# Operand tiles on multiples of 512 bytes, and an expert layer's routing arithmetic in smaller pieces

## Chip, cores and metric

One of the cores of a Trainium2 chip runs the kernel. The metric is the time of one execution on the device, in microseconds (us). The kernel before takes 1301.25 us, the median of 3 runs (1300.66 to 1303.61).

## The reference

A trunk of two layers over 272 tokens (16 meta tokens and 256 of the input) of 1024 features, all in float32:

```python
for i in range(DEPTH):
    hn = rms_norm(h, mix_norm_g[i])
    h = h + (conformer_conv(hn, ...) if i % 2 == 0 else multiscale_pool(hn, ...))
    hn = rms_norm(h, ffn_norm_g[i])
    h = h + (swiglu(hn, ...) if i % 2 == 0 else moe_swiglu(hn, ...))
return rms_norm(h[:, N_META:], final_norm_g)
```

Layer 0 has a convolution module (two projections around a depthwise convolution of 31 taps) and a dense SwiGLU of width 2816. Layer 1 has a pooling mixer and a mixture of experts: a router picks the best 2 of 8 experts for each token, each expert is a SwiGLU of width 3584, and the two results are added with softmax weights. The experts' weights are 352 MB of the 402 MB that the weight queue loads.

## The kernel before

**Precision.** TensorE multiplies in a form of float32 that keeps fewer bits (float32r). A weight tile `raw` of 2048 columns (1 MB) is therefore cut in two units of 1024; ScalarE casts each into `w_hi` (line 105, `Weights.hi`), and VectorE subtracts, `w_lo = raw - w_hi` (line 128, `Weights.lo`). Activations are split likewise, and a product is three matmuls: high by high, low by high, high by low. A few units of the experts are left `plain`: they are multiplied straight from `raw` as float32.

**Dense part.** In layer 0 the weights are the stationary operand and the activations the moving one. `xh` and `xl` (lines 317 and 318) hold 8 chunks of 272 columns, one behind the other, 1088 bytes each; `sh` and `slo` (line 539) and `gh` and `gl` (line 631, 11 chunks each) do the same for later stages. `column` (line 336) multiplies one tile of weights with all chunks by `mm3` (line 311, whose matmuls are lines 313 to 315).

**Expert part.** Here the tokens of an expert are stationary (`x0b` to `x6b` for the big experts 0 to 4 with room for 128 tokens, `x0s` to `x6s` for the small ones 5 to 7 with room for 64) and 512 columns of weights move. The work is 56 steps, one for each expert and each 512 of its 3584 columns, listed in `steps` (line 220): the first 7 are expert 0's (of which the first `ALONE` = 6 and the last `QUIET` = 3 of all steps are fixed as big ones), then steps of big and small experts mostly alternate. A step projects to gate and up (`project`, line 1156, matmuls in lines 1167, 1171 and 1173), and between them does the down projection of the step before (`down`, line 1228, lines 1236 to 1239; `weave`, line 1429). A step of a big expert has 36 + 24 matmuls of 512 columns and 4 float32 ones, one of a small expert 32 + 16.

**The order of the side work.** `side` (line 1141) is a list of small functions. `beside` (line 1143) is called after every second chunk of a projection and every second of a down projection, that is 10 times in a step (6 times in step 0, which has no step before it): it frees a weight unit, runs the first function of `side`, and then writes the subtraction of the next units to VectorE's queue. So a function of `side` stands on VectorE between two `w_lo` subtractions, and its length decides how late the next one is. At most 4 cast units are ahead (`W_BUFS`). In each step one slot goes to the low part of the turned activations (`flip_later`, line 1198, puts it in front).

The experts 1 to 7 are ordered by how many tokens they have: `places` (line 902) ranks them and writes their numbers (`ids_i`), `count_most` (line 920) the largest count, `by_place` (line 931) reorders positions and weights, and `weights_of_tokens` (line 948) makes the softmax weights. Then for each expert `assign` builds a matrix P of ones and zeros (line 1005), `factors` multiplies it with the tokens' factors (line 1075), and `known` copies the result out. In step 0 the slots hold: factors and ranking of expert 0's and all places (slots 1 and 2), the counts (slot 3), the weights (4), the assign of expert 1 (5), its factors (6). At the start of step `SUMS_FROM` = 4, six functions are put in front of the list: for each half t of the tokens the sum of high and low features (line 1386) and `gains(t)` (line 1372: four products into the one buffer `x_of`, then a store to `x_rows` in HBM from POOL's queue), then `freed`, then `rows_of_tokens` (line 959, 14 instructions). POOL gathers the rows of a later expert from `x_rows` (`fetch`, lines 1019 and 1347); that of expert 5 (`BIG`) at the start of step 5.

SP issues all weight loads in the order in which their buffers are freed (line 85). It reads the experts' numbers into registers at step `IDS_AT` = 1 (line 1358); all engines read the largest count at step `COUNT_AT` = 2.

Of the kernel before, what the change touches and what calls it, by code (L numbers as in the profile page):

```python
# [6 lines left out]
F32 = mybir.dt.float32  # L7
F32R = mybir.dt.float32r
# [4 lines left out]
OP = mybir.AluOpType  # L13
# [5 lines left out]
T = SEQ + META  # L19
# [17 lines left out]
DG, SOONER, SUMS_LAG = 8, 12, 2  # L37
ABOUT = 5
LINE = 16
ALONE, IDS_AT, COUNT_AT, SUMS_FROM, QUIET = 6, 1, 2, 4, 3  # L40
PLAIN_AT = 6
BIG, CAP, SMALL_CAP = 5, 128, 64
TURN_AT = {False: 4, True: 2}
# [123 lines left out]
def body(tc, xT, w_pw1, w_pw2, w_gu, w_dn, w_pool, m_gate, m_up, m_down, small, moe_g,  # L167
# [7 lines left out]
    def pool(stack, name, bufs=1, **kw):  # L175
        return stack.enter_context(tc.tile_pool(name=name, bufs=bufs, reuse_waits="tile", **kw))
# [101 lines left out]
    for t in iw[1:]:  # L278
# [5 lines left out]
    POOL.iota(token[:, :2], pattern=[[128, 2]], base=0, channel_multiplier=1,  # L284
              allow_small_or_imprecise_dtypes=True)
    g1 = consts.tile([128, KC], F32)

    def table(func):

# [24 lines left out]
        PE.matmul(ps, lhsT=w[0], rhs=x[1], start=False, stop=False)  # L314
        PE.matmul(ps, lhsT=w[1], rhs=x[0], start=False, stop=last)  # L315

    xh = act.tile([128, KC, T], F32R, name="xh")
    xl = act.tile([128, KC, T], F32R, name="xl")
    rstd = act.tile([128, T], F32, name="rstd")
    ssq = act.tile([128, T], F32, name="ssq")  # L320

    def split(hi, lo, src):
        ACT.copy(hi, src)
# [40 lines left out]
    with ExitStack() as cs:  # L364
# [5 lines left out]
        pstat = pool(cs, "cst", 1, space=PSUM)  # L370
        u = cv.tile([128, KC, T], F32, name="u")
        v = cv.tile([128, KC, T], F32, name="v")

        warm(psum.tile([128, T], F32, name="mm")[:, :128], WARM[5])
        table(AF.Sqrt)
# [160 lines left out]
        sums()  # L536
        dgs.close()
        sx = pool(cs, "sx", side="right")
        sh = sx.tile([128, KC, T], F32R, name="sh")
        slo = sx.tile([128, KC, T], F32R, name="slo")  # L540

        d2 = tmp.tile([128, T], F32, name="hn")
        ACT.activation(d2, mu, AF.Square)
# [81 lines left out]
    with ExitStack() as cs:  # L625
# [2 lines left out]
        psum = pool(cs, "fps", 3, space=PSUM)  # L628
        pstat = pool(cs, "fst", 1, space=PSUM)
        ppool = pool(cs, "fpt", 2, space=PSUM)  # L630
        gh = ff.tile([128, FH, T], F32R, name="gh")
        gl = ff.tile([128, FH, T], F32R, name="gl")
        ms = pstat.tile([128, T], F32, name="ms")
        sl = {}

# [43 lines left out]
        for s in range(2):  # L679
# [7 lines left out]
            for m in range(KC):  # L687
# [24 lines left out]
                if s == 1 and m in POOL_AFTER[:-1]:  # L712
# [11 lines left out]
        rst = po.tile([128, 3], F32, name="rst")  # L724
        rsqrt(rst, st, 0, ff, 3)
        yh, yl = (t.rearrange("p k t -> p (k t)")[:, :2 * D].rearrange("p (b d) -> p b d", b=2)
                  for t in (xh, xl))
        def weigh(g, src):

            d = slice(g * 256, g * 256 + 256)  # L730
# [171 lines left out]
    def places(scratch):  # L902
# [17 lines left out]
    def count_most(scratch):  # L920
        hot, cmp = (squares_of(scratch, i, 1)[:, 0] for i in range(2))
        most = scratch[:, 0:1]
        shape = [128, n_rest, n_rest]
# [5 lines left out]
        DVE.tensor_copy(cnt_i, most)  # L929

    def by_place(dst, src, scratch):

# [12 lines left out]

    wt = rt.tile([128, 2, 2], F32, name="wt")

    def weights_of_tokens(scratch):
        den = rt.tile([128, 2], F32, name="den")
        DVE.tensor_scalar(den, ex, 1.0, None, op0=OP.add)  # L950
        DVE.reciprocal(wt[:, :, 0], den)
        DVE.tensor_mul(wt[:, :, 1], wt[:, :, 0], ex)
        for t in range(2):
            DVE.tensor_scalar(rc[:, t], oh[:, t, 0], wt[:, t, 0:1], None, op0=OP.mult)
            DVE.scalar_tensor_tensor(rc[:, t], oh[:, t, 1], wt[:, t, 1:2], rc[:, t],
                                     op0=OP.mult, op1=OP.add)
        by_place(rcq[:, :, :, 2], rc, scratch)

    def rows_of_tokens(scratch):


        small, room = (scratch[:, i * NE:(i + 1) * NE] for i in range(2))
        has, row = (scratch[:, 32 + 16 * i:48 + 16 * i].rearrange("p (t e) -> p t e", t=2)
                    for i in range(2))
        t4, t4b = (scratch[:, 64 + 32 * i:96 + 32 * i].rearrange("p (t k e) -> p t k e", t=2, k=2)
                   for i in range(2))
        r4, m4 = (scratch[:, 128 + 4 * i:132 + 4 * i].rearrange("p (t k) -> p t k", t=2)
                  for i in range(2))
        s2, s4 = [128, 2, NE], [128, 2, 2, NE]
        DVE.tensor_scalar(small, place_of, float(BIG), None, op0=OP.is_ge)  # L970
# [3 lines left out]
        DVE.scalar_tensor_tensor(room, small, float(BIG * (CAP - SMALL_CAP) - CAP), room,  # L974
                                 op0=OP.mult, op1=OP.add)
        DVE.scalar_tensor_tensor(row, posm, -1.0, room[:, None].to_broadcast(s2),
                                 op0=OP.add, op1=OP.add)
        DVE.tensor_scalar(small, place_of, float(BIG - 1), None, op0=OP.not_equal)
        DVE.tensor_tensor(has, has, small[:, None].to_broadcast(s2), op=OP.mult)
        DVE.tensor_tensor(t4, oh, has[:, :, None].to_broadcast(s4), op=OP.mult)  # L980
# [53 lines left out]
    class Expert:  # L1034
# [47 lines left out]
        def fetch(self, rows):  # L1082
            self.rows = rows
            fetch_rows(rows, self.q, self.width)
# [49 lines left out]

    with ExitStack() as cs:
        ws = pool(cs, "mw", 2)
        pm = pool(cs, "mpm", 2, space=PSUM)
        pg_pool = pool(cs, "mpg", 1, space=PSUM)
        pu_pool = pool(cs, "mpu", 1, space=PSUM)
# [185 lines left out]
        for i, t in enumerate(gain1):  # L1325
            nc.gpsimd.dma_start(t, bass.AP(tensor=moe_g.tensor, offset=moe_g.offset + i * 256,
                                           ap=[[0, 128], [1, 256]]))
        table(AF.Silu)
        side += [lambda: experts[0].factors(2),
                 lambda: (experts[0].known(2), places(scratch)),  # L1330
                 lambda: (count_most(scratch), by_place(posq, posm, scratch)),
                 lambda: weights_of_tokens(scratch)]
        before = lambda: None
        for q in range(1, NE):
            e = experts[q] = Expert(q, ws, pm)
            side += [lambda e=e, before=before: (before(), e.assign(posq)), e.factors]
            before = e.known
            if q == BIG - 1:
                before = lambda e=e: (e.known(), e.back())
        side.append(before)  # L1340
# [4 lines left out]
        prev, py_of, n_fetched = None, {}, 0  # L1345

        def fetch(q):
            experts[q].fetch(fetched_rows[n_fetched % 2])

        for n_step, (q, f) in enumerate(steps):  # L1350
            e = experts[q]
# [16 lines left out]
            if n_step == SUMS_FROM:  # L1368
# [15 lines left out]
                pieces = []  # L1384
                for t in range(2):
                    pieces += [lambda t=t: DVE.tensor_add(yacc[:, t], xth[:, t].bitcast(F32),
                                                          xtl[:, t].bitcast(F32)),
                               lambda t=t: gains(t)]
# [202 lines left out]
```

## Time and profile before

| | before |
|---|---|
| time, median of 3 runs | 1301.25 us |
| the profiled execution: its time, and its span from first to last instruction | 1302.38 us, 1300.2 us |
| TensorE matmuls, share of the span | 98% |
| VectorE, ScalarE | 84%, 71% |
| moved to and from HBM, mean | 318 GB/s |
| granted clock of TensorE, mean | 0.994 |

A row of the profile names the engine (PE is TensorE, DVE is VectorE, ACT is ScalarE, POOL is GpSimd; PEld its weight loads; SPq and the like the queues' own instructions), the line of the kernel, the operation, and the tiles written and read. Matmuls are pipelined, so that the time from one start to the next, not the length given for one, is what a matmul takes of TensorE. "<-" names what ended a wait.

### The profile page before, as it was taken

Reading aid. Unit: us, or ns where it says so; the run is one execution under the profiler, and the core shown is the slowest. Engines: PE = TensorE matmul, PEld = TensorE weight load, DVE = VectorE, ACT = ScalarE, POOL = GpSimd, SP = SyncE. Lnnn points to the kernel's source line nnn. Section 1 sums busy time; section 2 is a strip of 40 time slices with the busy share of each in tenths; the row PEclk is TensorE's granted clock in tenths of the full one; section 3 lists DMA queues with packets and bytes.
Section 4 is the critical chain, followed back from the end, with each engine's and each line's share of the span. In section 5 each row is a group of like instructions: output and inputs, shape, how many; then the busy total and the mean of one; then the engine's idle time right before and its main releaser. Section 6 shows DMA issues by size and latency. Waiting matters only on the chain.

```text
span 1300.2 us, 19132 instructions
## 1 busy us (share of the span) xinstructions
PE 1272.4 (98%) x6655; PEld 1038.2 (80%) x6655; DVE 1096.6 (84%) x1471; ACT 927.5 (71%) x1263; POOL 22.4 (2%) x37
## 2 busy tenths in 40 slices
PE   9999999999989999999999999999999999999995
PEld 8988999999977767777777777777777777777773
DVE  7997886666677788999899998899989998999876
ACT  6765644445564657888688878888878887888764
POOL 0000000000010010000000000000000000000010
PEclk9999999999998999999999999999999999999998
DMA  9800435523867889999999799999999999999971
GB/s 364 310 15 1 142 134 199 203 88 139 317 251 282 319 325 366 419 420 420 409 410 413 283 406 421 420 421 420 419 377 392 422 420 422 374 422 421 419 298 36
DMA packets 61401, 414.22 MB, mean 319 GB/s; under 512 B 6896, under 2 KB 7536, under 8 KB 14320
## 3 DMA queue, kind: packets, MB, share of 16 engines
q1 hardware_dynamic: 58032, 402.22, 77.4%
q0 software_dynamic: 1872, 6.55, 1.4%
q10 hardware_dynamic: 1392, 4.14, 0.8%
q8 instruction: 54, 0.88, 0.3%
q14 instruction: 51, 0.42, 0.1%
HBM read 407.90 MB, written 4.98 MB: 318 GB/s over the span
## 4 chain that ended last, share of the span: by engine, by line
PE 91%; DVE 3%; DMA 3%; ACT 1%; issue 1%; SPq 0%; ACTq 0%; DVEq 0%
PE pu L1167 11%; PE pg L1167 10%; PE mm L315 7%; PE mm L313 7%; PE mm L314 7%; PE pg L1173 6%; PE pu L1173 6%; PE pyb L1239 5%; PE pyb L1236 5%; PE pyb L1238 5%; PE mm L515 4%; PE pg L1171 4%; PE pu L1171 3%; PE pys L1236 3%; PE pys L1239 3%; PE m L1196 2%
## 5 line engine op out<-in xcount | busy, mean ns | idle before, releaser
L128 DVE TENSOR_TENSOR w_lo<-raw,w_hi 128x1024 fp32r<-128x1024 f32 (+1 forms) x704 | 819.3, 1202 | 121.5 <-ACT w_hi L105 113.4
L105 ACT CAST w_hi<-raw 128x1024 fp32r<-128x1024 f32 (+1 forms) x704 | 707.3, 1034 | 239.2 <-PE mm L314 73.9
L315 PE MATMUL mm<-xh,w_lo 128*128 128x272 f32 x480 | 139.4, 290 | 0.5 <-DVE w_lo L128 0.5
L313 PE MATMUL mm<-xh,w_hi 128*128 128x272 f32 x480 | 139.6, 291 | 0.3 <-ACT xh L327 0.3
L314 PE MATMUL mm<-xl,w_hi 128*128 128x272 f32 x480 | 139.0, 290 | 0.1
L1236 PE MATMUL pyb<-w_hi,hh 128*128 128x512 f32 x272 | 112.6, 414 | 0.0
L1239 PE MATMUL pyb<-w_lo,hh 128*128 128x512 f32 x272 | 108.9, 400 | 2.2 <-DVE w_lo L128 2.2
L1238 PE MATMUL pyb<-w_hi,hl 128*128 128x512 f32 x272 | 107.4, 395 | 0.0
L314 PEld LDWEIGHTS mm<-xl,w_hi 128*128 128x128 f32 x480 | 90.5, 188 | 1.2 <-DVE xl L330 0.6
L315 PEld LDWEIGHTS mm<-xh,w_lo 128*128 128x128 f32 x480 | 90.3, 188 | 1.3 <-DVE w_lo L128 0.7
L313 PEld LDWEIGHTS mm<-xh,w_hi 128*128 128x128 f32 x480 | 90.3, 188 | 0.5 <-ACT xh L327 0.4
L1236 PE MATMUL pys<-w_hi,hs 128*128 128x512 f32 x168 | 74.2, 442 | 0.0
L1167 PE MATMUL pu<-raw,x6b 128*128 128x512 f32 x140 | 67.7, 607 | 0.0
L1239 PEld LDWEIGHTS pyb<-w_lo,hh 128*128 128x128 f32 x272 | 51.2, 188 | 19.7 <-DVE w_lo L128 7.8
L1239 PE MATMUL pys<-w_lo,hs 128*128 128x512 f32 x168 | 66.3, 395 | 0.0
L1167 PE MATMUL pg<-raw,x6b 128*128 128x512 f32 x140 | 65.8, 592 | 0.0
L1238 PEld LDWEIGHTS pyb<-w_hi,hl 128*128 128x128 f32 x272 | 51.3, 188 | 13.4 <-issue 2.4
L1236 PEld LDWEIGHTS pyb<-w_hi,hh 128*128 128x128 f32 x272 | 51.2, 188 | 12.7 <-ACT w_hi L105 2.2
L409 DVE SCALAR_TENSOR_TENSOR v<-u,sm,v 128x271 f32<-128x271 f32 (+29 forms) x137 | 55.5, 478 | 0.0
L313 PE MATMUL mm<-gh,w_hi 128*128 128x272 f32 x176 | 50.7, 288 | 0.0
L315 PE MATMUL mm<-gh,w_lo 128*128 128x272 f32 x176 | 50.7, 288 | 0.0
L314 PE MATMUL mm<-gl,w_hi 128*128 128x272 f32 x176 | 50.5, 287 | 0.0
(405 smaller groups left out, 2341.1 us busy)
## 6 DMA issues: line engine op xcount, KB each, us to landing
raw<-m_gate SPq DMA_DIRECT2D x112, 1024.0 KB, 14.8
raw<-m_up SPq DMA_DIRECT2D x112, 1024.0 KB, 10.0
raw<-m_down SPq DMA_DIRECT2D x111, 1024.0 KB, 17.3
raw<-w_gu SPq DMA_DIRECT2D x22, 1024.0 KB, 4.9
raw<-w_dn SPq DMA_DIRECT2D x16, 704.0 KB, 4.0
raw<-w_pw SPq DMA_DIRECT2D x10, 1024.0 KB, 15.2
y_rows<-rows ACTq DMA_DIRECT2D x4, 512.0 KB, 5.3
h<-xT SPq DMA_DIRECT2D x4, 272.0 KB, 4.5
```

Of the source, the lines that this page charges most:

```text
L105: self.nc.scalar.copy(hi[:, :n], self.raw[i][:, s:s + n])
L128: self.nc.vector.tensor_sub(lo, self.raw[i][:, s:s + n], hi.bitcast(F32))
L313: PE.matmul(ps, lhsT=w[0], rhs=x[0], start=first, stop=False)
L314: PE.matmul(ps, lhsT=w[0], rhs=x[1], start=False, stop=False)
L315: PE.matmul(ps, lhsT=w[1], rhs=x[0], start=False, stop=last)
L409: DVE.scalar_tensor_tensor(v[:, c, j:], u[:, c, :T - j], w, v[:, c, j:], op0=OP.mult, op1=OP.add)
L1167: PE.matmul(ps, lhsT=hi, rhs=w[0][:, i], start=(k == 0), stop=(k == KC - 1 and len(w) == 1))
L1171: PE.matmul(ps, lhsT=x[k - i][:, i, n:], rhs=w[0][:, i], start=False, stop=False)
L1173: PE.matmul(ps, lhsT=hi, rhs=w[1][:, i], start=False, stop=(k == KC - 1))
L1236: PE.matmul(ps, lhsT=a, rhs=wh[:, j % 2], start=first, stop=False)
L1238: PE.matmul(ps, lhsT=b[0], rhs=wh[:, j % 2], start=False, stop=False)
L1239: PE.matmul(ps, lhsT=a, rhs=wl[:, j % 2], start=False, stop=last)
```

## The change

Addresses. Unused tiles (`to_a_line`) are put in front of pools, so that what follows starts elsewhere: 192 bytes in `consts`, ahead of the pools of `raw`, `w_hi` and `w_lo`; 128 bytes in the experts' work pool `mw`; 32 bytes in `sx` and `ff`. The chunks of `xh`, `xl`, `sh`, `slo`, `gh`, `gl` are spaced by TP = 288 columns (1152 bytes), of which 272 are used. `rstd` moves to two other pools.

Side work. `places`, `count_most`, `by_place` and `weights_of_tokens` become one generator, `ranked`, in 7 pieces, one a slot; `rows_of_tokens` becomes 3 pieces. The factors of an expert share a slot with the assign of the next, two slots behind its own assign. The six functions of step 4 become a list of 12 entries with pauses, put behind the list at step 3; the gather of expert 5 is one of them. With its slots counted out the list runs: step 0 the factors and `known` of expert 0 and pieces 1 to 4; step 1 pieces 5 to 7 and the first assigns and factors; step 2 the rest of them; step 3 the first sum, `gains(0)`, the second sum and `freed`; step 4 `gains(1)`, the gather and the 3 pieces of `rows_of_tokens`.

```diff
+TP = T + LINE
-ALONE, IDS_AT, COUNT_AT, SUMS_FROM, QUIET = 6, 1, 2, 4, 3
+ALONE, IDS_AT, COUNT_AT, SUMS_FROM, QUIET = 6, 1, 2, 3, 3
...
     g1 = consts.tile([128, KC], F32)
+    consts.tile([128, 3 * LINE], F32, name="to_a_line")
...
-    xh = act.tile([128, KC, T], F32R, name="xh")
-    xl = act.tile([128, KC, T], F32R, name="xl")
-    rstd = act.tile([128, T], F32, name="rstd")
-    ssq = act.tile([128, T], F32, name="ssq")
+    xs = [act.tile([128, KC, TP], F32R, name=n) for n in ("xh", "xl")]
+    xh, xl = (t[:, :, :T] for t in xs)
+    ssq = act.tile([128, TP], F32, name="ssq")[:, :T]
...
-        sh = sx.tile([128, KC, T], F32R, name="sh")
-        slo = sx.tile([128, KC, T], F32R, name="slo")
+        sx.tile([128, 8], F32, name="to_a_line")
+        sh, slo = (sx.tile([128, KC, TP], F32R, name=n)[:, :, :T] for n in ("sh", "slo"))
...
-        gh = ff.tile([128, FH, T], F32R, name="gh")
-        gl = ff.tile([128, FH, T], F32R, name="gl")
+        ff.tile([128, 8], F32, name="to_a_line")
+        rstd = ff.tile([128, T], F32, name="rstd")
+        gh, gl = (ff.tile([128, FH, TP], F32R, name=n)[:, :, :T] for n in ("gh", "gl"))
...
+    def in_pieces(steps):
+
+        return [lambda: next(steps, None)] * 9
+
+    def ranked(scratch):
...
+        yield
         DVE.scalar_tensor_tensor(key, counts, float(NE), slots[:, :NE], op0=OP.mult,
                                  op1=OP.subtract)
...
+        yield
         DVE.tensor_tensor(hot, place[:, None, :].to_broadcast(shape),
...
+        yield
+        by_place(posq, posm, scratch)
+        yield
+        den = rt.tile([128, 2], F32, name="den")
...
+        yield
+        by_place(rcq[:, :, :, 2], rc, scratch)
...
     with ExitStack() as cs:
         ws = pool(cs, "mw", 2)
+        ws.tile([128, 2 * LINE], F32, name="to_a_line", bufs=1)
...
-        side += [lambda: experts[0].factors(2),
-                 lambda: (experts[0].known(2), places(scratch)),
-                 lambda: (count_most(scratch), by_place(posq, posm, scratch)),
-                 lambda: weights_of_tokens(scratch)]
-        before = lambda: None
+        pause = lambda: None
+        ranking = ranked(scratch)
+        next(ranking)
+        side += [lambda: experts[0].factors(2), lambda: experts[0].known(2)] + in_pieces(ranking)[:7]
         for q in range(1, NE):
-            e = experts[q] = Expert(q, ws, pm)
-            side += [lambda e=e, before=before: (before(), e.assign(posq)), e.factors]
-            before = e.known
+            experts[q] = Expert(q, ws, pm)
...
+        for q in range(1, NE + 1):
+            side += [lambda q=q: (q > 1 and experts[q - 1].factors(),
+                                  q < NE and experts[q].assign(posq)),
+                     lambda q=q: q > 1 and known(q - 1)]
...
-                side[:0] = pieces + [freed, lambda: rows_of_tokens(temp)]
+                placing = rows_of_tokens(temp)
+                next(placing)
+                side += [lambda: whole(0), pause, lambda: gains(0), pause, lambda: whole(1), freed,
+                         pause, pause, lambda: gains(1), pause, lambda: fetch(BIG),
+                         pause] + in_pieces(placing)[:3]
...
-            if n_step + 1 in after_of and n_step > SUMS_FROM:
+            if n_step + 1 in after_of and n_step + 1 >= ALONE:
                 fetch(after_of[n_step + 1])
-                n_fetched += 1
-            if n_step in after_of and n_step - 1 <= SUMS_FROM:
-                fetch(after_of[n_step])
-                n_fetched += 1
```

## Rows read from the trace of the kernel before

**Rows 1.** The page, part 1: busy us (share of the span), instructions.

```profile
PE 1272.4 (98%) x6655; PEld 1038.2 (80%) x6655; DVE 1096.6 (84%) x1471; ACT 927.5 (71%) x1263; POOL 22.4 (2%) x37
```

**Rows 2.** The page, part 4: the chain that ended last, by engine.

```profile
PE 91%; DVE 3%; DMA 3%; ACT 1%; issue 1%; SPq 0%; ACTq 0%; DVEq 0%
```

**Rows 3.** Windows: us, busy us of each engine (instructions), granted clock, DMA share, GB/s.

```profile
390.07:396.89 6.82, 5.72 (x12) 3.36 (x13) 4.56 (x10) 0.00 (x0) 0.00 (x0) 0.50 0.54 183
396.89:434.66 37.77, 37.77 (x168) 28.72 (x167) 27.91 (x47) 22.68 (x25) 0.00 (x0) 1.00 0.85 314
434.66:493.50 58.84, 55.79 (x226) 39.92 (x224) 47.34 (x65) 35.78 (x41) 3.41 (x4) 1.00 0.88 332
493.50:1257.74 764.24, 762.32 (x3241) 578.94 (x3240) 689.68 (x699) 627.64 (x753) 10.15 (x9) 1.00 0.98 404
```

**Rows 4.** Timeline of PE, steps 53 and 54: start us, us, what.

```profile
1222.11 0.39 PE L1167 MATMUL pg<-w_hi,x0b 128*128 128x512 f32 x1
...
1224.66 0.40 PE L1173 MATMUL pg<-w_lo,x2b 128*128 128x512 f32 x1
...
1239.93 0.39 PE L1167 MATMUL pg<-w_hi,x0b 128*128 128x512 f32 x1
```

**Rows 5.** The chain in order of time: start us, us, what; steps 12 and 14.

```profile
590.87 1.72 PE pg L1167 x4
...
620.88 1.72 PE pg L1167 x4
```

**Rows 6.** Waits of ACT, 497 to 1255 us: total us, times, longest us.

```profile
ACT w_hi L105 <- DMA raw<-m_down: 0.5, 1, 0.5
```

**Rows 7.** DMA queues: the weights' queue; packets, MB, share of 16 engines.

```profile
q1 hardware_dynamic: 58032, 402.22, 77.4%
```

**Rows 8.** Timeline of PE, step 0.

```profile
387.65 0.40 PE L1173 MATMUL pu<-w_lo,x4b 128*128 128x512 f32 x1
391.17 1.01 PE L1075 MATMUL m<-rcq,P 128*128 128x3 f32 x4 [3.12 <-DVE P L1005]
```

**Rows 9.** Timeline of DVE, step 0: first and last of the ranking's 27 instructions.

```profile
382.42 0.16 DVE L907 SCALAR_TENSOR_TENSOR scratch<-counts,slots 128x8 f32<-128x8 f32 x1
...
389.63 0.16 DVE L938 COPY rcq<-rc 128x2 f32<-128x2 f32 x1
```

**Rows 10.** Timeline of PE, end of step 4 and start of step 5.

```profile
467.72 0.39 PE L1238 MATMUL pyb<-w_hi,hl 128*128 128x512 f32 x1
469.47 0.50 PE L1239 MATMUL pyb<-w_lo,hh 128*128 128x512 f32 x1 [1.36 <-DVE w_lo L128]
...
472.12 0.39 PE L1171 MATMUL pg<-w_hi,x0b 128*128 128x512 f32 x1
474.20 0.50 PE L1173 MATMUL pg<-w_lo,x0b 128*128 128x512 f32 x1 [1.69 <-DVE w_lo L128]
```

**Rows 11.** Timeline of DVE, steps 4 and 5.

```profile
456.93 1.43 DVE L1376 TENSOR_TENSOR x_of<-raw,gain 128x256 f32<-128x256 f32 x4
...
466.85 1.43 DVE L1376 TENSOR_TENSOR x_of<-raw,gain 128x256 f32<-128x256 f32 x4 [3.35 <-DMA x_rows<-x_of]
...
470.47 0.17 DVE L970 TENSOR_SCALAR scratch<-place_of 128x8 f32<-128x8 f32 x1
...
472.86 0.15 DVE L985 TENSOR_TENSOR share<-wt,scratch 128x4 f32<-128x4 f32 x1
```

**Rows 12.** Timeline of POOL, start of step 5.

```profile
472.30 1.02 POOL L1019 DMA_INDIRECT rows<-x_rows,at  x1 [3.19 <-PE pyb L1239]
```

**Rows 13.** Timeline of PE, dense SwiGLU: first of 12 matmuls and the one behind them.

```profile
181.49 0.29 PE L313 MATMUL mm<-xh,w_hi 128*128 128x272 f32 x1
...
183.00 0.29 PE L313 MATMUL mm<-xh,w_hi 128*128 128x272 f32 x1
```

**Rows 14.** Timeline of PE, pooling mixer: the second of two bands of 256 columns.

```profile
356.55 0.28 PE L776 MATMUL po<-band,xl 128*128 128x256 f32 x1
356.67 0.22 PE L777 MATMUL po<-band,xh 128*128 128x128 f32 x1
```

More of the change, by code (lines that the diff above doesn't have):

```diff
@@ L372, in body @@
         v = cv.tile([128, KC, T], F32, name="v")
+        rstd = cv.tile([128, T], F32, name="rstd")
         warm(psum.tile([128, T], F32, name="mm")[:, :128], WARM[5])
@@ L726, in body @@
         yh, yl = (t.rearrange("p k t -> p (k t)")[:, :2 * D].rearrange("p (b d) -> p b d", b=2)
-                  for t in (xh, xl))
+                  for t in xs)
         def weigh(g, src):
@@ L900, in squares_of @@
         return t.rearrange("p (t q e) -> p t q e", t=n, q=n_rest)
-    def places(scratch):
+    def in_pieces(steps):
+        return [lambda: next(steps, None)] * 9
+    def ranked(scratch):
         hot, cmp = (squares_of(scratch, i, 1)[:, 0] for i in range(2))
@@ L918, in places @@
         DVE.tensor_copy(ids_i, place)
-    def count_most(scratch):
-        hot, cmp = (squares_of(scratch, i, 1)[:, 0] for i in range(2))
+        yield
         most = scratch[:, 0:1]
-        shape = [128, n_rest, n_rest]
         DVE.tensor_tensor(cmp, hot, counts[:, None, 1:].to_broadcast(shape), op=OP.mult)
@@ L929, in count_most @@
         DVE.tensor_copy(cnt_i, most)
+        yield
+        by_place(posq, posm, scratch)
+        yield
+        den = rt.tile([128, 2], F32, name="den")
+        DVE.tensor_scalar(den, ex, 1.0, None, op0=OP.add)
+        DVE.reciprocal(wt[:, :, 0], den)
+        DVE.tensor_mul(wt[:, :, 1], wt[:, :, 0], ex)
+        yield
+        for t in range(2):
+            DVE.tensor_scalar(rc[:, t], oh[:, t, 0], wt[:, t, 0:1], None, op0=OP.mult)
+            DVE.scalar_tensor_tensor(rc[:, t], oh[:, t, 1], wt[:, t, 1:2], rc[:, t],
+                                     op0=OP.mult, op1=OP.add)
+        yield
+        by_place(rcq[:, :, :, 2], rc, scratch)
     def by_place(dst, src, scratch):
@@ L946, in body @@
     wt = rt.tile([128, 2, 2], F32, name="wt")
[L948 to L957, printed above, removed]
     def rows_of_tokens(scratch):
@@ L969, in rows_of_tokens @@
         s2, s4 = [128, 2, NE], [128, 2, 2, NE]
+        yield
         DVE.tensor_scalar(small, place_of, float(BIG), None, op0=OP.is_ge)
@@ L975, in rows_of_tokens @@
                                  op0=OP.mult, op1=OP.add)
+        yield
         DVE.scalar_tensor_tensor(row, posm, -1.0, room[:, None].to_broadcast(s2),
@@ L979, in rows_of_tokens @@
         DVE.tensor_tensor(has, has, small[:, None].to_broadcast(s2), op=OP.mult)
+        yield
         DVE.tensor_tensor(t4, oh, has[:, :, None].to_broadcast(s4), op=OP.mult)
@@ L1328, in body, with known @@
         table(AF.Silu)
-        side += [lambda: experts[0].factors(2),
-                 lambda: (experts[0].known(2), places(scratch)),
-                 lambda: (count_most(scratch), by_place(posq, posm, scratch)),
-                 lambda: weights_of_tokens(scratch)]
-        before = lambda: None
+        pause = lambda: None
+        ranking = ranked(scratch)
+        next(ranking)
+        side += [lambda: experts[0].factors(2), lambda: experts[0].known(2)] + in_pieces(ranking)[:7]
         for q in range(1, NE):
-            e = experts[q] = Expert(q, ws, pm)
-            side += [lambda e=e, before=before: (before(), e.assign(posq)), e.factors]
-            before = e.known
+            experts[q] = Expert(q, ws, pm)
+        def known(q):
+            experts[q].known()
             if q == BIG - 1:
-                before = lambda e=e: (e.known(), e.back())
-        side.append(before)
+                experts[q].back()
+        for q in range(1, NE + 1):
+            side += [lambda q=q: (q > 1 and experts[q - 1].factors(),
+                                  q < NE and experts[q].assign(posq)),
+                     lambda q=q: q > 1 and known(q - 1)]
         after_of = {ALONE - 1: BIG}
@@ L1344, in body @@
                 after_of[n_step] = q + 1
-        prev, py_of, n_fetched = None, {}, 0
+        prev, py_of, n_fetched = None, {}, []
         def fetch(q):
-            experts[q].fetch(fetched_rows[n_fetched % 2])
+            experts[q].fetch(fetched_rows[len(n_fetched) % 2])
+            n_fetched.append(q)
         for n_step, (q, f) in enumerate(steps):
@@ L1382, in freed, with whole @@
                         rows += [tile[:, i] for i in range(2)]
[L1384 to L1388, printed above, removed]
-                temp = ws.tile([128, 256], F32, name="scratch", tag="ut", bufs=1)
-                side[:0] = pieces + [freed, lambda: rows_of_tokens(temp)]
+                def whole(t):
+                    DVE.tensor_add(yacc[:, t], xth[:, t].bitcast(F32), xtl[:, t].bitcast(F32))
+                temp = ws.tile([128, 256], F32, name="scratch", tag="ut", bufs=1)
+                placing = rows_of_tokens(temp)
[3 more added lines that the diff above has]
+                         pause] + in_pieces(placing)[:3]
             if n_step == len(steps) - 1:
```

## The prediction, made before the change was run

> **What bounds the kernel now.** I read the page first: TensorE is busy for 98% of the span [rows 1], and the chain of work that ended last runs through it for 91% [rows 2]. A busy TensorE need not be the limit, so the next view is a table of windows [rows 3]: from 493.5 us to the last step the DMA engines are busy 98% at 404 GB/s and DVE 690 of 764 us, so three engines stand close together there. Before that, from 390 to 493.5, the DMA share is 0.54 to 0.88 and TensorE has holes.
>
> The steps tell which of the three sets the pace. A step of a big expert alone lasts 17.82 us from first matmul to first matmul [rows 4], and a big and a small step together 30.01 us [rows 5]; both figures repeat to 0.05 us wherever nothing disturbs them, and adding up the matmuls of a pair gives the same 30 us. Between 497 and 1255 us only one cast of ScalarE waits for a weight tile, for 0.5 us [rows 6]. Adding up the packets of the weight queue [rows 7] tile by tile, a tile takes 2.488 us while the queue is full, lands every time at least 11.5 us ahead of its cast, and a pair's 12 tiles need 29.86 us. So TensorE leads, with DMA 0.5% behind and a stock of some 11.5 us of tiles: what TensorE saves in the mixed steps is a gain up to that stock and no further. What it saves before 490 us passes through, since there the tiles are issued as TensorE frees them and DMA has idle time.
>
> **Part one: small pieces.** The ranking's 27 VectorE instructions stand in three lumps between step 0's w_lo subtractions, from 382.42 to 389.79 us [rows 9]; the first assign of P comes behind them, and the factors' matmul waits for it. TensorE goes from 387.65 to 391.17 [rows 8]; a matmul takes 0.23, so 3.29 us are lost. In that hole the granted clock drops to 1.2 GHz, from 390.07 to 396.89 [rows 3]; the first 1.10 us of that are still hole, the other 5.72 us do work that takes half as long at 2.4 GHz: 2.86 us. Sum 6.15 us. With the change assign stands in the tenth slot and the factors in the twelfth, two slots apart, step 0 carries four pieces of about 1 us or less, and its VectorE work falls to some 11 of 12 us. The moved pieces go to steps 1 and 2, which carried assigns and copies already; VectorE is busy there for 27.9 of 37.8 us [rows 3], which is the cover.
>
> The second hole: w_lo late at 469.47, 1.52 us past its place, and again at 474.20, 1.85 us [rows 10]. Ahead of the first, the second group of four products into x_of waits 3.35 us for the store of the first, whose products end at 458.36 [rows 11]: that store is done only 8.5 us later. Ahead of the second stand the 14 instructions from 470.47 to 473.01 in one lump. The change puts six slots, over 10 us at 17.8 us for ten slots, between the two groups, and splits the lump in three pieces of under 1 us. Sum 3.37 us. Both parts: 9.5 us. The bounds: 6.2 if small waits of 0.3 us or so take the place in the ten or so slots, 10.3 if all that steps 0 to 5 take beyond their own matmuls goes.
>
> The queues it is moved past. SP reads the experts' numbers at step 1 and every engine the count at step 2; the numbers now come with the fourth slot and not the second, still 5 us ahead of that point. POOL's gather for expert 5 left at 472.30 after two stores [rows 12], at the start of the step that uses it; it now stands in the middle of step 4, behind the second store, which POOL waits out for some 8.5 us; nothing else is queued on POOL. Its rows arrive by my count 6 us ahead of their transposes: no cost, no gain.
>
> **Part two: addresses.** I add up the tiles' bytes in the order of allocation. The weight tiles (moving) of the expert steps stood 320 bytes past a multiple of 512, the tokens (stationary) 192; both go to 0. In the dense part the weights go to 0 as well, and the activations' chunks, spaced 1088 bytes, alternate between multiples of 128 and odd multiples of 64; spaced 1152 and moved, all stand on multiples of 128.
>
> Dense: 12 matmuls take 1.51 us [rows 13], 126 ns each. Grouped by start address over the dense stage, the gap from one to the next is 125.89 ns on the mean of 2,127, but 124.65 where both start on multiples of 128 and 127.37 where both are on odd 64s. All 2,160 at the lower value: 1.24 x 2,160 = 2.7 us, on the path. The Trainium skill, "SBUF — State Buffer", section "Specifications (TRN2)", gives lines of 16 bytes and a penalty only for stepping from one to the next; by that rule every chunk stood on whole lines already, the dense gain is 0 and the sum ends 2.7 us higher. The trace contradicts it by 2.7 ns a matmul, so I go by the trace.
>
> Expert steps: 11 matmuls of 512 columns take 2.55 us [rows 4], 232 ns each, 0.453 ns a column. Both bounds come from the dense rows. If an operand's start on an odd 64 costs, 3,116 matmuls win 2.7 ns each, 8.4 us, or by columns 5.1 ns, 16 us. If its end on a multiple of 128 costs (the odd chunks, 1088 long, end there), these matmuls, which end on an odd 64 now, will lose as much. I take 0: 272 columns at 124.65 are 0.458 a column, and 256 columns that start on no multiple of 64 at all (the band, 96 past 512) take 0.12 us [rows 14], 0.457 a column; so the 512s already run at the rate of the well-placed ones.
>
> **The sum.** The profiled execution took 1302.38 us around a span of 1300.2, 1.1 above the runs' median. 1302.4 - 9.5 - 2.7 = 1290.2; against the median 1289. A difference under 0.2% (2.6 us) can't be told from none.
>
> **The rivals.**
> - *The excess of the expert matmuls goes.* 512 columns at 2.4 GHz are 213 ns, and rows 4 show 232. If the placing of both operands together is what costs (no matmul of before has both on 512), steps 0 to 21 win 1,212 x 17 = 20 us, and from there DMA holds it to its stock of 11.5 us and 0.15 us for each of some 17 pairs: 14. With 12.2 from above: 1255. For it: the slope is 9% over one column a clock. Against: so is that of every float32r matmul of before, however placed. The Trainium skill, "TensorE: Matmul & The Clock Gate", section "Back-to-back issue gap", puts the gap at N/2.4 + 2.5 ns, 216 for 512; by that the whole excess is a loss to be won and the time is 1256 (an estimate). The trace does not agree for any float32r matmul here. 14%.
> - *The start costs*, as above: 8.4 to 16 us more, 1273 to 1281. For it the dense classes, against it the 256s. 16%.
> - *The pieces bring waits of their own*: w_lo is late by some tenths in many slots, or a pause is too short and x_of waits again. 4 to 7 us come back: 1293 to 1296. 12%.
> - *Slower.* The end costs: all 3,116 expert matmuls end on a multiple of 128. By columns 5.1 x 3,116 = 16 us, more than the 12.2 won: 1289 + 16 = 1305 at that price. It decides from 4.8 ns a matmul (12.2 + 2.6 us over 3,116); at 2.7 ns it leaves 1297. 7%, of it 5% over the bound.
> - *It does not do what it says*: the classes in the dense part hang on something else, and the addresses change nothing: 1291.5. 7%.
>
> **How the numbers follow.** The forecast has 44%, with 1285 to 1294 of its own from the bounds. The range of 8 in 10 takes in the forecast, the rivals of the start, the pieces and the addresses (79%), and leaves out most of the first and the slower one: 1266 to 1298. Faster by over 0.2% is 0.88, same 0.07, slower 0.05.
>
> **What would show it.** Right: no wait of the factors for P, no drop of the granted clock between 377 and 400, step 0 under 13 us, steps 4 and 5 at 17.8 and 19.5 us; 12 dense matmuls in 1.496 us; 11 expert matmuls still in 2.55 us and pairs at 30.0. Wrong: pairs below 29.8 us with casts waiting for DMA (the first rival), 11 expert matmuls in 2.60 (the slower one), or DVE's w_lo as a releaser of TensorE in steps 0 to 5.

## The result, and the profile after

The changed kernel took 1283.49 us (median of four, 1283.19 to 1291.91), the kernel before beside it 1301.53 (four, 1300.66 to 1303.61): a ratio of 0.9872, with a 95% interval of 0.9836 to 0.9908. The forecast was 1289.0, in a range of 1266 to 1298. In the execution that was profiled first TensorE's clock stood at 1.2 GHz for 17.1 us in the pooling mixer, which made it some 8 us longer (1291.91) than the other three, so the rows below are of a second profile of the same kernel (the run after_again, 1284.46 us, span 1282.2).

The windows of that second profile: steps 0; 1 to 3; 4 to 6; 7 to 54 (columns as in [rows 3]):

```profile
376.84:389.19 12.35, 12.07 (x49) 8.56 (x49) 9.32 (x33) 9.76 (x12) 0.00 (x0) 1.00 0.53 201
389.19:445.93 56.74, 56.74 (x249) 42.98 (x247) 48.63 (x85) 34.29 (x37) 0.55 (x1) 1.00 0.89 326
445.93:501.47 55.54, 55.54 (x234) 40.67 (x232) 45.03 (x63) 37.02 (x45) 5.20 (x5) 1.00 1.00 382
501.47:1239.81 738.34, 736.38 (x3162) 561.92 (x3161) 674.78 (x684) 615.28 (x737) 7.49 (x7) 1.00 0.98 409
```

TensorE's busy time fills every window from step 1 to 6, and the clock is 1.00 throughout, where [rows 3] had holes and a stretch at 0.50. Against the first matmuls of the same steps in the profile of before:

```
us                       before    after    difference
start of step 0          376.76    376.84     +0.08
steps 0 to 6             135.43    124.63    -10.80
  step 0                  18.06     12.35     -5.71
  step 1                  21.14     18.96     -2.18
  step 2                  18.70     20.04     +1.34
  step 3                  17.81     17.74     -0.07
  step 4                  19.42     17.60     -1.82
  step 5                  21.60     19.46     -2.14
  step 6                  18.69     18.48     -0.21
steps 7 to 54            745.55    738.34     -7.21
step 55 to the end        42.46     42.39     -0.07
span                    1300.2    1282.2     -18.0
```

There are two gains: 10.8 us in the first seven steps, and 7.2 spread evenly over the other 48. Up to step 0, the dense stage included, nothing changed. The page's parts 1 (TensorE) and 4, against [rows 1, 2]:

```profile
PE 1260.6 (98%) x6655; PEld 1033.8 (81%) x6655; DVE 1094.6 (85%) x1471; ACT 927.9 (72%) x1263; POOL 22.1 (2%) x37
PE 92%; DMA 4%; DVE 2%; ACT 1%; issue 1%; SPq 0%; ACTq 0%; DVEq 0%
```

TensorE still sets the time, and VectorE's share of the chain fell from 3% to 2%. All waits of TensorE from 377 to 502 us (us in total, times, longest):

```profile
PE pg L1181 <- DVE x2b L1081: 0.6, 1, 0.6
PE m L1088 <- DVE rcq L965: 0.3, 1, 0.3
```

Of the waits of before in this stretch, P's (3.12) and the two for w_lo (1.36 and 1.69) are gone [rows 8, 10]; the two that are left were there before. TensorE at the place of [rows 8]:

```profile
387.65 0.39 PE L1187 MATMUL pu<-w_lo,x4b 128*128 128x512 f32 x1
387.88 1.88 PE L1181 MATMUL pu<-raw,x6b 128*128 128x512 f32 x4
389.19 0.79 PE L1181 MATMUL pg<-w_hi,x0b 128*128 128x512 f32 x1
```

Right behind the last w_lo matmul of step 0 comes the next product; the factors, which stood in between and waited, now follow P two slots later, in step 1. VectorE, at the place of [rows 9] and at that of the second lump [rows 11]:

```profile
388.50 1.23 DVE L129 TENSOR_TENSOR w_lo<-raw,w_hi 128x1024 fp32r<-128x1024 f32 x1
389.64 0.25 DVE L956 TENSOR_TENSOR scratch<-posm,scratch 128x98 f32<-128x98 f32 x1
389.93 0.25 DVE L958 TENSOR_REDUCE posq<-scratch 128x14 f32<-128x98 f32 x1
390.10 0.16 DVE L959 COPY posq<-posm 128x2 f32<-128x2 f32 x1
390.17 1.22 DVE L129 TENSOR_TENSOR w_lo<-raw,w_hi 128x1024 fp32r<-128x1024 f32 x1
...
438.18 1.42 DVE L1395 TENSOR_TENSOR x_of<-raw,gain 128x256 f32<-128x256 f32 x4
...
448.13 1.43 DVE L1395 TENSOR_TENSOR x_of<-raw,gain 128x256 f32<-128x256 f32 x4
```

A piece of 0.5 us now stands between two w_lo, and the second x_of comes 10 us behind the first and waits for nothing. The first gather, expert 5's, left 13.8 us earlier than in [rows 12], after 8.16 us of idle time in which POOL did nothing else (its timeline):

```profile
458.55 1.55 POOL L1032 DMA_INDIRECT rows<-x_rows,at  x1 [8.16 <-PE pyb L1253]
460.41 1.27 POOL L1032 DMA_INDIRECT rows<-x_rows,at  x1 [0.30 <-issue]
```

A big and a small step, and 11 matmuls of 512 columns in step 54 (the chain in order of time, against [rows 5], and TensorE's timeline, against the 11 of step 53 in [rows 4]):

```profile
579.40 1.72 PE pg L1181 x4
...
609.18 1.72 PE pg L1181 x4
```

```profile
1222.21 0.39 PE L1181 MATMUL pg<-w_hi,x0b 128*128 128x512 f32 x1
...
1224.71 0.39 PE L1187 MATMUL pg<-w_lo,x2b 128*128 128x512 f32 x1
```

29.78 us a pair (before 30.01), and 2.50 us for 11 matmuls (before 2.55). The dense stage, against [rows 13]:

```profile
180.84 0.29 PE L315 MATMUL mm<-xh,w_hi 128*128 128x272 f32 x1
...
182.36 0.29 PE L315 MATMUL mm<-xh,w_hi 128*128 128x272 f32 x1
```

12 matmuls in 1.52 us, no less than the 1.51 of before.

### The profile page after: what moved, and what is told of

Its sections match the earlier page's. It is cut to its first block, busy times and chain, and to the rows that moved or that the text cites. A ratio compares the mean times of both kernels' runs of the same rounds, so it can differ in the third digit from the quotient of the medians.

```text
span 1289.8 us, 19132 instructions
## 1 busy us (share of the span) xinstructions
PE 1268.5 (98%) x6655; PEld 1041.8 (81%) x6655; DVE 1095.4 (85%) x1471; ACT 927.8 (72%) x1263; POOL 24.1 (2%) x37
## 4 chain that ended last, share of the span: by engine, by line
PE 92%; DMA 4%; DVE 2%; ACT 1%; issue 1%; SPq 0%; ACTq 0%; DVEq 0%
PE pu L1181 11%; PE pg L1181 11%; PE mm L317 7%; PE mm L315 7%; PE mm L316 7%; PE pu L1187 6%; PE pg L1187 6%; PE pyb L1253 5%; PE pyb L1250 5%; PE pyb L1252 5%; PE mm L517 4%; PE pu L1185 4%; PE pg L1185 4%; PE pys L1250 3%; PE pys L1253 3%; PE m L1210 2%
## 5 line engine op out<-in xcount | busy, mean ns | idle before, releaser
L1250 PEld LDWEIGHTS pyb<-w_hi,hh 128*128 128x128 f32 x272 | 51.1, 188 | 11.5 <-ACT w_hi L106 2.2
## 6 DMA issues: line engine op xcount, KB each, us to landing
raw<-m_gate SPq DMA_DIRECT2D x112, 1024.0 KB, 13.8
```

Source lines behind the costliest of these rows:

```text
L1250: PE.matmul(ps, lhsT=a, rhs=wh[:, j % 2], start=first, stop=False)
```

## The experiments

**The two parts, each alone.** The kernel before with the pieces and every address as it was (pieces), the kernel before with the addresses and the lumps (addresses), and the changed kernel again beside them (after_again).

> The changed kernel once more, as the standard for the parts beside it. In its first profile the granted clock stood at 1.2 GHz for 17.1 us in the pooling mixer and the logits (about 361 to 378 us), where the kernel before had 2.4; that execution took 1291.9 us, its four others 1283.2 to 1283.7. Theory: that drop belongs to single executions and not to the change; then the median is 1283.5, and where the profile has no drop there, the first step starts at about 377 us and the span is about 1282. Rival: the change brings the drop with it in a good share of the executions; then several of the runs stand near 1291.

> The kernel before with the small pieces alone, every address as before. Theory (the two parts add up): steps 0 to 6 together fell from 135.4 to 124.6 us, and some 540 matmuls of 512 columns at 3.3 ns less are 1.8 of these 10.8, so the stalls are worth 9.0 us: 1301.5 - 9.0 = 1292.5, with 126.4 us for steps 0 to 6, no drop of the clock at 390 to 397 us, and 512-column matmuls still at 232.5 ns. Rival (the pieces are the whole gain, and the quicker matmuls go along with less work of the other engines beside them): 1283.5 to 1286, gap 229. Rival (the holes go only since TensorE's pace changed): over 1296.

> The kernel before with the addresses alone, the ranking and the scaled features in lumps as before. Theory: 512-column matmuls at 229.2 ns in place of 232.5, steps 7 to 54 at 738.5 us in place of 745.6, and in steps 0 to 6 1.8 us less: 8.9 us, the dense stage unchanged at 126 ns a matmul (no gain there): 1292.5. The holes at steps 0, 4 and 5 stay as long as before. Rival (the addresses change nothing and the pieces are the whole gain): 1300 to 1302. Rival (waits behind the lumps take part of it back): 1294 to 1297.

```
pieces:     the diff without its lines on to_a_line, TP, xs, rstd, ssq, sh, slo, gh, gl, yh
addresses:  those lines of the diff alone
```

Measured: after_again 1284.5 us (0.988 of before, 0.986 to 0.991), pieces 1292.6 (0.994; 0.992 to 0.996), addresses 1293.1 (0.992; 0.991 to 0.994), before 1302.55. Against that the pieces are worth 9.95 us and the addresses 9.45, together 19.4; both at once gave 18.1, so they add up to within 1.3 us. By the stages of the traces:

```
us                      before   pieces   addresses   both
steps 0 to 6            135.43   125.79    134.88    124.63
steps 7 to 54           745.55   745.51    738.53    738.34
gap of 512 columns, ns  232.47   232.46    229.05    228.99
```

The gap is the time from one float32r matmul's start to the next one's, the mean over neighbours in the program with no wait between them (under 260 ns; some 2,700). Each part does its own work and nothing of the other's. In the kernel with the lumps steps 0 to 6 keep about half of what their matmuls save (0.55 us, where pieces and both differ by 1.16). Of the 0.61 that is missing, 0.20 is in the waits: TensorE arrives sooner and waits longer for VectorE (for P 3.21 us, before 3.12; for the two w_lo 3.16 together, before 3.05). And 0.36 is the clock: the drop comes 0.7 us later after the start of step 0 than before, so that 6.45 us of matmuls fall into it and not 5.72 [rows 3]. The wait for P and the window of the drop in addresses:

```profile
390.73 1.01 PE L1078 MATMUL m<-rcq,P 128*128 128x3 f32 x4 [3.21 <-DVE P L1008]
```

```profile
390.35:397.18 6.83, 6.45 (x13) 4.00 (x14) 4.06 (x10) 0.00 (x0) 0.00 (x0) 0.50 0.58 173
```

**Which addresses.** The prediction gave the expert stage nothing. Four theories could explain the 3.4 ns: the place where an operand starts, whole spans of 512, the weights alone or the tokens alone, and the distance between the two. The first run moves both operands by 64 bytes.

```diff
-    consts.tile([128, 3 * LINE], F32, name="to_a_line")
+    consts.tile([128, 4 * LINE], F32, name="to_a_line")
```

> The changed kernel with weights and tokens both 64 bytes past a multiple of 512, and all else alike. Theory S (an operand that starts on an odd multiple of 64 costs some 3 ns): the 512-column matmuls are back at 232 to 233 ns and the time at 1283.5 + 7 to 9 = 1290.5 to 1292.5; in the dense stage, where the weights are the stationary operand, little changes. Theory D (what counts is the distance between the two operands, the same here as in the changed kernel): 229 ns and 1283.5. Theory W (whole spans of 512 bytes count, whatever the step): 232 ns or more, and the next run at 128 bytes will tell it from S.

Measured: 1282.5 us, gap 228.9. Both operands stood on odd multiples of 64 and the gain stayed, so neither the start nor whole spans decide. Four more runs move one operand against the other; in the changed kernel, for x384, x256 and weights_alone in this line,

```diff
-        ws.tile([128, 2 * LINE], F32, name="to_a_line", bufs=1)
+        ws.tile([128, 6 * LINE], F32, name="to_a_line", bufs=1)
```

with 6 for x256, 5 for weights_alone, the whole line gone for x384; for tokens_alone the line in consts gone and 5 here.

> The changed kernel, with the tokens 384 bytes past a multiple of 512 and the weights on one: each stands on a multiple of 128, and the weights are 128 past the tokens, as in the kernel before (320 and 192). Theory D (the distance between the two operands counts): the 512-column matmuls are back at 232.5 ns, steps 7 to 54 at 745.5 us and the time near 1292.5. Theory P (each operand's own place counts, and any multiple of 128 or the like does): 229 ns, 738.4 us, 1283.5.

> The changed kernel, with the tokens 256 bytes past a multiple of 512 and the weights on one. Theory D with a period of 512: 231 ns or more, steps 7 to 54 over 742 us. Theory D with a period of 256 or less, and theory P: 229 ns, 738.4 us and 1283.5.

> The changed kernel, with the tokens 192 bytes past a multiple of 512 as in the kernel before and the weights on one. Theory D: what the distance of 320 does, the same here as where the tokens alone are moved; between 229 and 233 ns. Theory P for the moving operand (the weights alone count): 229 ns and 1283.5. Theory P for the stationary operand: 232.5 ns and 1292.5; but then tokens 64 past, in the run before, would have been slow, and were not.

> The changed kernel, with the weights 320 bytes past a multiple of 512 as in the kernel before and the tokens on one. Theory D: the same gap as where the weights alone are moved, to 0.5 ns. Theory P for the moving operand: 232.5 ns and near 1292.5; for the stationary operand: 229 ns and 1283.5.

The fifth takes the kernel before and moves both from there, at the same distance; what it says of the dense stage comes next.

```diff
     g1 = consts.tile([128, KC], F32)
+    consts.tile([128, 3 * LINE], F32, name="to_a_line")
```

> The kernel before with 192 bytes put ahead of the weight tiles and nothing else: every weight tile goes from 320 to 0 past a multiple of 512, the tokens from 192 to 384, so that the distance between the two operands of an expert matmul stays 128, while in the dense stage the weights (stationary) move by 192 against the activations (moving), which stay. Expert stage, theory D (distance): 232.5 ns, steps 7 to 54 at 745.5 us, and about the time of before, 1301 to 1303; theory P (multiples of 128 and 512 for their own sake): 229 ns and 1293. Dense stage: in the kernel before a gap from a chunk on a multiple of 128 was 124.8 ns and from an odd 64 127.0, with the distance to the next weights odd in the first case and even in the second. If the start of the moving operand counts, the two classes stay so; if the distance counts, they change places.

All of them, by the places of the weight tiles (moving) and of the tokens (stationary) past a multiple of 512 bytes, added up from the tiles' sizes in the order of allocation; the distance is weights less tokens:

```
run            weights  tokens  distance   gap, ns  a pair   steps 7   time
                                mod 256                us    to 54     us
before             320     192      128     232.47   30.01    745.55   1302.5
consts_alone         0     384      128     232.44   30.03    745.57   1301.4
x384                 0     384      128     232.41   29.99    745.62   1292.3
weights_alone        0     192       64     229.60   29.81    740.02   1286.6
tokens_alone       320       0       64     229.46   29.81    739.73   1284.4
after_again          0       0        0     228.99   29.78    738.34   1284.5
x256                 0     256        0     228.93   29.74    738.25   1283.9
shift64             64      64        0     228.93   29.71    737.99   1282.5
```

(Before and consts_alone have the lumps, the others the pieces, so the times compare within each of the two; the gaps and steps 7 to 54 compare throughout.) Rows at one distance agree to 0.15 ns, whatever the two places are, and x384, on multiples of 128 throughout, is as slow as before. So it is the distance between the moving and the stationary operand, taken by 256 bytes, that the gap follows: 128 costs 3.5 ns over 0, and 64 costs 0.6; a distance of 192 was not run. All stationary tiles of a run's expert steps stand at one place past a multiple of 256, so these runs cannot tell a matmul's own stationary operand from that of the next one, which is loaded meanwhile (PEld is busy for 81% of the span, beside PE's 98%); why the distance costs anything is not shown. In the chain, a pair of x384 and one of shift64:

```profile
580.90 1.72 PE pg L1180 x4
...
610.89 1.72 PE pg L1180 x4
```

```profile
578.00 1.72 PE pg L1181 x4
...
607.71 1.72 PE pg L1181 x4
```

**The dense stage.** Its 2,160 matmuls have the activations moving and the weights stationary. Grouped by the distance of the two by 256 bytes (ns, some 515 to 1,070 matmuls each):

```
run           chunks every  weights at   0      64     128    192    all
before              1088       320     126.8  124.8  127.2  124.9  125.89
consts_alone        1088         0     126.8  124.8  127.2  124.6  125.83
after_again         1152         0     125.5     -   126.3     -   125.88
shift64             1152        64        -   125.2     -   125.7  125.42
tokens_alone        1152       320        -   125.2     -   125.7  125.42
```

From before to consts_alone the weights move and the chunks stay. By distance the four classes are the same to 0.3 ns; by the chunk's own start they change places: chunks on multiples of 128 went from 124.8 to 127.0, those on odd 64s from 127.0 to 124.7. So here too the distance counts and not the start. It is not all that counts: a chunk has three matmuls, and at one distance they differ more than the classes do. For chunks 0 and 4 of the tiles `xh` and `xl` they take 129.8, 120.2 and 124.3 ns before; in consts_alone the chunks that now stand at that distance, 3 and 7, take 129.9, 120.1 and 124.4, so the whole pattern moves along with the distance. The change puts every chunk into the two classes that were dear. They measure 125.5 and 126.3 there, less than before (why is open; the spacing changed with them), and the mean comes out where it was. In shift64 and tokens_alone all stand at odd multiples of 64 apart, 0.46 ns less a matmul, 1.0 us over the 2,160. The start of step 0 does not settle that 1.0: it lies between 374.9 and 377.2 us in the profiles with the changed addresses that have no drop of the clock ahead of it.

**The clock behind the hole.** In the kernel before, ones times ones on TensorE while it waits for P:

```diff
             self.f = self.pm.tile([128, 512], F32, name="m")
+            if self.q == 1:
+                warm(self.f[:, :128], 44)
```

> The kernel before with 44 matmuls of ones by ones (bfloat16, 128 columns, some 0.065 us each, 2.9 us) on TensorE ahead of the factors' first matmul of the second expert, in the hole of step 0: the hole stays, but TensorE is not idle in it. Theory (the clock drop behind the hole is a cost of its own): no stretch at 1.2 GHz at 390 to 397 us, step 0 and the start of step 1 2.9 us shorter, 1302.5 - 2.9 = 1299.6. Rival (the drop comes from something else, or the ones only lengthen the hole): 1302 to 1305.

Measured over twelve runs: 1299.3 us, 0.998 of before (0.996 to 0.999): 2.8 us. TensorE's timeline, and the window at the place of the drop in [rows 3]:

```profile
387.24 2.63 PE L309 MATMUL m<-ones 128*128 128x128 bf16 x44
390.50 0.61 PE L1077 MATMUL m<-rcq,P 128*128 128x3 f32 x4 [0.64 <-DVE P L1005]
390.97 1.96 PE L1169 MATMUL pu<-raw,x6b 128*128 128x512 f32 x4
```

```profile
390.07:396.89 6.82, 6.38 (x31) 4.81 (x32) 5.63 (x12) 2.40 (x3) 0.00 (x0) 1.00 0.81 296
```

P comes when it came before, the clock stays at 2.4 GHz, and steps 0 and 1 take 36.41 us in place of 39.20. The drop is a cost of its own behind the hole: 2.8 us (1.4 to 4.7 by the interval), where the prediction had 2.86.

**The ranking's pieces without the features'.** In the changed kernel, the scaled features and rows in lumps again.

```diff
-                side += [lambda: whole(0), pause, lambda: gains(0), pause, lambda: whole(1), freed,
-                         pause, pause, lambda: gains(1), pause, lambda: fetch(BIG),
-                         pause] + in_pieces(placing)[:3]
+                side[:0] = [lambda: whole(0), lambda: gains(0), lambda: whole(1), lambda: gains(1),
+                            freed, lambda: list(placing)]
```

(with SUMS_FROM = 4 and the gather for BIG at the start of step 5)

> The changed kernel with the tokens' scaled features and rows in lumps at the head of step 4 again, and expert 5's gather at the start of step 5: the addresses and the ranking's pieces alone. Theory: the holes of steps 4 and 5 come back, 3.4 us: 1284.0 + 3.4 = 1287.4, steps 0 and 1 as in the changed kernel (12.35 and 18.96 us), steps 4 and 5 at 19.3 and 21.4. Rival (the features' pieces pay for the ranking's, which crowd steps 1 and 2): under 1285, or over 1290.

Measured: 1289.35 us by the median of four that lie far apart (1286.8 to 1296.2), so the time settles little; the profiled one took 1287.0. Steps 0 and 1 stay at 12.37 and 18.97 us; steps 4 and 5 take 21.40 and 19.93, 41.3 together against 37.1. The waits of the two holes came back as one, behind x_of (VectorE's and TensorE's timelines), and the clock fell behind it:

```profile
459.41 1.43 DVE L1395 TENSOR_TENSOR x_of<-raw,gain 128x256 f32<-128x256 f32 x4 [3.75 <-DMA x_rows<-x_of]
```

```profile
462.04 0.50 PE L1253 MATMUL pyb<-w_lo,hh 128*128 128x512 f32 x1 [1.96 <-DVE w_lo L129]
```

```profile
462.48:465.89 3.41, 3.41 (x10) 2.66 (x9) 3.07 (x16) 1.04 (x1) 1.02 (x1) 0.50 0.83 264
```

1.96 us of wait and 1.70 of clock (half of 3.41) are 3.7 of the 4.3. The two sets of pieces work each for itself, as the theory had it, but the place of the hole and the clock in it were not foreseen.

**Both operands 64 bytes past.** shift64 took 1282.5 us (0.986 of before, 0.984 to 0.988) beside 1284.5 for the changed kernel on the same chip. The intervals overlap, so it is not shown to be faster; the one sign of it is the dense gap, by which 1.0 us would be expected.

## Why the prediction was right, and where not

**The forecast came out 5.5 us high.** It had 9.5 us from the pieces and 2.7 from the addresses; the traces show 9.6 and 8.4. The pieces were right; of the addresses only the sign was, with the gain in the stage to which the prediction gave none, and none in the stage to which it gave 2.7. That 1283.49 lies in the range is in part luck: it is below the 1285 to 1294 that the forecast had of its own, and the range reached further down for rivals, of which the nearest in price (the start costs) had its reason refuted.

*Part one, 9.5 us: right, step by step.* In the kernel with the pieces alone steps 0 to 6 lost 9.64 us. Of it steps 0 to 3 lost 6.07 (18.06 to 12.43, 21.14 to 19.12, 18.70 to 20.19, 17.81 to 17.90) where the prediction had 6.15, and steps 4 and 5 3.56 (19.42 to 17.81, 21.60 to 19.65) where it had 3.37. The 2.86 for the clock are the 2.8 of warm_hole. Of the signs named, no wait for P, no drop of the clock, step 0 under 13 us (12.35), steps 4 and 5 near 17.8 and 19.5 (17.60 and 19.46) all came; w_lo releases TensorE nowhere in steps 0 to 5. The rival that the pieces bring waits of their own finds no row. The cover held: VectorE is busy for 48.6 of the 56.7 us of steps 1 to 3. One margin was reckoned too wide: the experts' numbers were written 3.7 us before SP read them (386.46 and 390.16), not 5, and TensorE waited for nothing of it.

*The gather: right in cost, not in margin.* It left 8.16 us behind the issue of the store, near the 8.5 reckoned, and its early start is worth nothing that a row shows. But the rows landed 3.8 us ahead of their transposes (467.45 and 471.27), not 6, and in before it was 4.8: the gather now took 8.9 us to land and not 4.6, and step 5 begins sooner too.

*Dense, 2.7 us: wrong, measured nothing.* The step that failed is "Grouped by start address". The classes were real, but all weights stood 320 past a multiple of 512, so that a chunk on a multiple of 128 was always at an odd distance from them, and the grouping could not tell the one from the other. consts_alone parts the two, and the distance has it. Moving the chunks and the weights at once took the good class away. The Trainium skill, "SBUF — State Buffer", section "Specifications (TRN2)", names lines of 16 bytes and a penalty for each step to a new one, and by that the dense sum came out right (no gain) where I went by the trace. As the whole rule the runs do not bear it out, since all these places are multiples of 16 and the gaps differ by 2.6 ns.

*Experts, 0: wrong, measured 7.2 us over steps 7 to 54 and 1.2 in steps 0 to 6.* The step that failed is "the 512s already run at the rate of the well-placed ones". It took 0.457 ns a column of the band of 256 columns as a well-placed rate, by the start of that operand alone, without the distance to its partner; the expert matmuls ran at 0.453 and now run at 0.447. With the waits in, a matmul of steps 7 to 54 gained 2.7 ns (244.7 to 242.0 on the mean of all 2,628), which is 7.1 of the 7.2 us.

*The rivals.* "The start costs" had the price nearly right (8.4 us at 2.7 ns for 3,116 matmuls) and the reason wrong: shift64 starts all on odd 64s at 1282.5. Its upper end, 1281, lies closer to the time than the forecast does. "The excess goes" had the reason nearly right, the placing of both operands together, and the price wrong: 3.5 ns a matmul and not 17, with gaps of 229 ns, not 213. The Trainium skill, "TensorE: Matmul & The Clock Gate", section "Back-to-back issue gap", gives N/2.4 + 2.5 ns for an isolated gap, 216 for 512; no run's mean for 512 columns is under 228.9. "The end costs" is refuted in the same table: x256 and after_again end on the multiples of 128 and are fast. "It does not do what it says" was right that the dense classes hang on something else, and wrong that the addresses then change nothing.

*The cap by DMA was not felt.* I had put a pair's tiles at 29.86 us; a pair takes 29.78 now, under the 29.8 named as a sign, but casts wait for tiles only twice from 490 us on, 0.8 us in all (before 0.5). Tiles land at least 11.6 us ahead of their casts (before 11.5, both by adding up the packets), and the transfers went along at 409 GB/s where [rows 3] had 404.

## What to carry to other kernels

Where a matmul's time varies with addresses, group it by the distance of the two operands and not by either one's place: a layout in which one operand is fixed shows the two as the same thing, and an edit that moves both can then lose what it gains. Pad tiles for that distance (here a multiple of 256 bytes for 512 columns, an odd multiple of 64 for 272), and leave round numbers alone that do nothing else. Small work that VectorE does beside a stream of casts belongs between them in pieces shorter than the slack of one; a hole in TensorE costs its length and then, where the clock falls behind it, about half of that stretch again.

## What was not expected of the hardware

- The gap of float32r matmuls follows the distance between moving and stationary operand by 256 bytes: for 512 columns 228.95 ns at 0, 229.5 at 64, 232.4 at 128. In the dense stage odd multiples of 64 are the quick ones (124.6 to 125.7 against 125.5 to 127.2). Why the order of 0 and 64 differs between the two, and why single gaps at distance 0 still lie between 224 and 236, stays open. Work beside them is not the cause in after_again: the gaps in which ScalarE or VectorE works throughout (90% and more of the gap) are 229.0 and 228.8 ns on the mean, those in which it rests 229.5 and 230.8.
- The clock fell to 1.2 GHz in the pooling mixer in single executions, with TensorE busy ahead of it, by the rows, on the bands' small matmuls as in [rows 14]. The first profile's window of that stretch, and the second's of the same time:

```profile
360.66:377.73 17.07, 16.71 (x75) 15.64 (x76) 9.24 (x26) 4.98 (x10) 5.31 (x8) 0.50 0.41 149
```

```profile
360.66:377.73 17.07, 15.19 (x133) 13.94 (x132) 12.76 (x44) 10.83 (x27) 4.23 (x8) 1.00 0.72 255
```

  Step 0 then started at 384.14 in place of 376.84, 7.3 us later. Times of that kind (7 to 8 us up, at a mean clock of 0.990 or less) came in 3 of the 11 executions of the changed kernel on record, in 3 of 46 of the kernel before and in 4 of 54 of all the others. Where the clock fell in those without a profile is not known, and whether the change makes them more frequent is not settled by that.
- The drop behind the hole of step 0 is itself not constant: 6.83 us long in the profiles of before and of addresses, 3.41 in consts_alone. At half the clock that is 1.7 us, which may be a part of the some 4 us by which the kernel before varies from one execution to the next; this was not tried.
